# S5 lags multiplied in the third MLP from maps read back, output maps stored in place, the inputs' factors made at once, stores by token of the chunk

## The chip, the cores and the metric

The kernel runs on one core of a Trainium2 chip. The metric is the device time of one execution in microseconds (us). The kernel before was timed in 3 runs: median 1107.81 us, from 1104.62 to 1108.13.

## The reference

A decoder trunk over 256 tokens of 1024 channels in float32. Four layers, each a mixer and a squared-ReLU MLP of 4096 hidden channels, each with a norm ahead and behind:

```python
h = h + rmsnorm(mixer(rmsnorm(h, g0)), g1)
h = h + rmsnorm(mlp(rmsnorm(h, g2)), g3)      # mlp: square(relu(x @ w_up)) @ w_down
```

The mixers are a gMLP, a multi-scale pooling, a multi-head latent attention and an S5 layer. In S5, 64 groups of 16 channels each drive a complex diagonal state of 64 values:

```python
mag = exp(lr * dt); ab_re = mag * cos(li * dt); ab_im = mag * sin(li * dt)
f_re = ((ab_re - 1) * lr + ab_im * li) / den; f_im = (ab_im * lr - (ab_re - 1) * li) / den
...
# state x[t] = ab * x[t-1] + (f * B) u[t];  y = Re(C x) + d_skip * u, then gelu and a GLU
```

Nothing of `ab`, `f`, their powers or their products with B and C depends on h, so a kernel can make them any time before S5.

## The kernel before

The residual h lives in SBUF as two blocks of 128 tokens. Every float32 product is made of three float32r products of high and low halves (`mm3`, shown by the names `zhi`, `zlo`, `h1hi`, `h1lo`). The weights stream from HBM in blocks of 1 MB on SP's queue into `raw` tiles; ACT writes the high half of a block (line 338), DVE the low half (line 339), into one of 8 `w` tiles. An MLP runs a head, then 7 groups; a group is one piece of 96 matmuls up (`mm<-zhi,w`) and two of 48 down (`acc<-w,h1hi`).

The order of instructions on each engine comes from a framework that schedules the program over a simulated time with priorities. The functions below give it units of work and times. `boundary` runs a sublayer's body, its norm behind (`post`, through `add_normed`, line 391), and lifts the next sublayer's input (transposes of the scaled h on PE, line 428). In `add_normed` DVE multiplies the accumulator with the gain (`t`, line 401), ACT sums its squares (`junk`, line 352), a chain of one-column operations gives the reciprocal root, and DVE updates h (line 405).

`Tables.work()` is a generator that runs beside the sublayers from the first MLP on. It builds what S5 needs. `maps()` (from line 1675) works on POOL through 16 chunks of two pairs of groups. For each it loads B and C (`bo`), transposed B (`bt`) and powers (`pb`), multiplies B with the factors f (operations 32 wide), copies the products into `cb`, multiplies C with eight powers (`e`), negates the imaginary half, stores `e` in `d_out`, and makes the input map (`f`, stored in `d_f`). After every second chunk `lags` multiplies `e` with `cb` on PE (names `pf<-e,cb`; 16 short passes) and ACT copies the result; `place` puts the result into a Toeplitz block and stores it in `d_lag`. At the end 8 transfers copy `d_lag` into `d_m`, and 4 copy `d_out` into `d_e` (line 1724), from DRAM to DRAM. `d_m`, `d_e` and `d_f` are what S5 loads as its weights. `k.drain()` in `emit` sees that all of this has been issued before the third MLP begins.

In the third MLP `reorder` stores h (`d_h`) and loads it back in chunk order (lines 451 and 453). `finish` (line 456) stores the output: for each block two halves of 512 channels, one from SP's queue and one from ACT's, each as 4 times 32 rows of 512 channels. POOL issues all the transfers of `Tables`, of `reorder` and of the norms' gains (`bc`, line 328), in one order.

## Time and profile before

| | |
|---|---|
| runs | 1104.62, 1108.13, 1107.81 us; median 1107.81 |
| profiled execution | 1106.46 us, span of the trace 1104.7 us |
| busy: PE, DVE, ACT, POOL | 1018.0, 736.8, 548.8, 381.2 us |
| mean granted clock of PE | 0.971 of full |

The order of the sublayers in the span: gMLP; first MLP with the boundary at its start near 102 us; pooling; second MLP from 322 us; attention; third MLP from 642 us; S5; fourth MLP from 914 us. PE is TensorE, DVE VectorE, ACT ScalarE, POOL GpSimd, SP SyncE. A row of the trace's timeline has start, duration, engine, line, operation, output and inputs, the number of equal instructions in sequence, and in brackets how long the engine had been idle before and what it waited for. "Idle <-X" means that X ended last among what was waited for.

### The profile page before, as it was taken

The numbers are of one execution on the slowest core, as the hardware profiler recorded it, in microseconds if no ns is written. First come the engines' busy times: TensorE is split into PE (matmuls) and PEld (weight loads), VectorE is DVE, ScalarE is ACT, GpSimd is POOL, SyncE is SP. The second block draws the span as 40 slices with busy tenths as digits, with TensorE's granted clock in tenths as the row PEclk, the third lists the DMA queues.
The fourth block names the chain that finished last, engine by engine and source line by source line (L and its number), as shares of the span: only waits on it lengthen the run. The fifth ranks groups of instructions, "written<-read, shape, count | busy, mean of one in ns | idle before, by whom it ended". The sixth has DMA issues, their size and how long they took to land.

```text
span 1104.7 us, 16412 instructions
## 1 busy us (share of the span) xinstructions
PE 1018.0 (92%) x6408; PEld 890.3 (81%) x6409; DVE 736.8 (67%) x1099; ACT 548.8 (50%) x826; POOL 381.2 (35%) x589
## 2 busy tenths in 40 slices
PE   7898999999679998998899879999998998999994
PEld 6796999898569897986777679899966777899983
DVE  5779999754896764666876555665658577464552
ACT  5946465453454443444555455554534556444531
POOL 5000001713779999999988530000000000000000
PEclk9999999999889998999999989999999999999998
DMA  9675465758576765665864699746477554546431
GB/s 334 220 250 191 153 213 207 234 197 299 171 243 232 252 211 203 217 216 174 252 201 149 193 388 266 267 164 217 158 292 297 189 169 159 207 163 219 155 113 38
DMA packets 82607, 233.97 MB, mean 212 GB/s; under 512 B 6321, under 2 KB 9649, under 8 KB 80737
## 3 DMA queue, kind: packets, MB, share of 16 engines
q1 hardware_dynamic: 67256, 182.73, 48.4%
q0 software_dynamic: 14720, 49.60, 13.6%
q8 instruction: 50, 0.82, 0.3%
q10 hardware_dynamic: 552, 0.59, 0.1%
q14 instruction: 29, 0.23, 0.1%
HBM read 218.48 MB, written 27.00 MB: 222 GB/s over the span
## 4 chain that ended last, share of the span: by engine, by line
PE 62%; POOL 14%; DVE 11%; DMA 4%; ACT 4%; issue 3%; SPq 0%; DVEq 0%; POOLq 0%; ACTq 0%
PE mm L296 30%; PE acc L296 30%; DVE w L339 3%; DMA raw<-in_a_w_in 2%; POOL tmp L1572 2%; DMA raw<-in_w_up 1%; POOL tmp L1569 1%; DVE h L405 1%; DMA d_f<-f 1%; PE pf L296 1%; ACT junk L352 1%; PE mm L428 1%; ACT w L338 1%; DVE w L337 1%; POOL e L1704 1%
## 5 line engine op out<-in xcount | busy, mean ns | idle before, releaser
L339 DVE TENSOR_TENSOR w<-raw,w 128x1024 fp32r<-128x1024 f32 (+3 forms) x308 | 383.1, 1273 | 165.9 <-ACT w L338 164.7
L338 ACT ACTIVATE w<-raw 128x1024 fp32r<-128x1024 f32 (+3 forms) x308 | 313.1, 1044 | 232.4 <-PE acc L296 126.9
L296 PE MATMUL acc<-w,h1hi 128*128 128x512 f32 (+1 forms) x1312 | 402.5, 390 | 4.1 <-ACT h1hi L338 3.4
L296 PE MATMUL mm<-zhi,w 128*128 128x256 f32 x1920 | 358.1, 286 | 4.3 <-DVE w L337 2.4
L296 PEld LDWEIGHTS mm<-zhi,w 128*128 128x128 f32 x1920 | 305.3, 194 | 8.4 <-DVE w L337 3.5
L296 PEld LDWEIGHTS acc<-w,h1hi 128*128 128x128 f32 x1312 | 244.9, 190 | 54.1 <-ACT h1hi L338 4.7
L296 PE MATMUL mm<-zlo,w 128*128 128x256 f32 x960 | 273.6, 285 | 0.0
L296 PE MATMUL acc<-w,h1lo 128*128 128x512 f32 (+1 forms) x656 | 253.4, 391 | 1.9 <-DVE h1lo L339 1.9
L296 PEld LDWEIGHTS mm<-zlo,w 128*128 128x128 f32 x960 | 186.0, 194 | 1.5 <-issue 0.4
L296 PEld LDWEIGHTS acc<-w,h1lo 128*128 128x128 f32 x656 | 124.5, 190 | 28.9 <-DVE h1lo L339 3.3
L628 DVE TENSOR_TENSOR s<-s 128x512 f32<-128x512 f32 x56 | 42.3, 756 | 61.4 <-ACT s L627 61.4
L627 ACT ACTIVATE s<-mm 128x512 f32<-128x512 f32 x56 | 33.4, 596 | 74.0 <-PE mm L296 72.0
L339 DVE TENSOR_TENSOR h1lo<-s,h1hi 128x512 fp32r<-128x512 f32 x60 | 53.9, 900 | 21.4 <-ACT h1hi L338 21.4
L338 ACT ACTIVATE h1hi<-s 128x512 fp32r<-128x512 f32 x60 | 45.2, 756 | 27.3 <-DVE s L628 25.6
L1272 POOL MEMSET t<- 128x32 f32 x2 | 0.3, 164 | 153.0 <-DVE h L405 153.0
L352 ACT ACTIVATE junk<-acc 128x512 bf16<-128x512 f32 x28 | 16.7, 595 | 57.1 <-DVE t L401 57.0
L296 PE MATMUL mm<-w,zhi 128*128 128x512 f32 x128 | 42.1, 412 | 2.6 <-DVE zlo L339 2.1
L401 DVE TENSOR_TENSOR t<-acc,bc 128x512 f32<-128x512 f32 x28 | 19.0, 686 | 37.5 <-PE acc L296 37.5
L296 PE MATMUL acc<-w,zhi 128*128 128x512 f32 (+2 forms) x128 | 38.7, 385 | 1.6 <-ACT w L336 1.6
L428 PE MATMUL mm<-ident,t 128*128 128x128 f32 x86 | 14.6, 309 | 25.8 <-DVE t L418 21.1
L328 POOL DMA_DIRECT2D bc<-in_norm_g x15 | 8.3, 556 | 77.6 <-DVE t L401 30.5
L428 PEld LDWEIGHTS mm<-ident,t 128*128 128x128 f32 x86 | 11.4, 159 | 29.0 <-issue 27.2
(310 smaller groups left out, 1207.8 us busy)
## 6 DMA issues: line engine op xcount, KB each, us to landing
raw<-in_w_up SPq DMA_DIRECT2D x64, 1024.0 KB, 5.3
raw<-in_w_down SPq DMA_DIRECT2D x64, 1024.0 KB, 5.1
bc<-in_norm_g POOLq DMA_DIRECT2D x15, 512.0 KB, 5.2
raw<-in_a_w_in SPq DMA_DIRECT2D x7, 1024.0 KB, 9.1
bt<-in_k_bt POOLq DMA_DIRECT2D x16, 256.0 KB, 3.8
raw<-in_a_w_out SPq DMA_DIRECT2D x4, 1024.0 KB, 4.9
d_out<-e POOLq DMA_DIRECT2D x16, 256.0 KB, 2.9
d_pb<-d_pw POOLq DMA_DIRECT2D x8, 512.0 KB, 9.6
```

The lines of the kernel that those rows point to most:

```text
L296: return self.nc.tensor.matmul(out, lhsT, rhs, start=start, stop=stop)
L337: return i, nc.vector.scalar_tensor_tensor(lo, src, gain, hi.bitcast(F32), op0=ALU.mult, op1=ALU.subtract)
L338: i = nc.scalar.activation(hi, src, AF.Copy)
L339: return i, nc.vector.tensor_tensor(out=lo, in0=src, in1=hi.bitcast(F32), op=ALU.subtract)
L352: self.nc.scalar.activation(self.junk[:, 0:x.shape[-1]], x, AF.Square, scale=scale, bias=shift, accum_out=ss[:, i:i + 1])
L401: nc.vector.tensor_tensor(tn, zn, gn, op=ALU.mult)
L405: nc.vector.scalar_tensor_tensor(hn, tn, q, hn, op0=ALU.mult, op1=ALU.add)
L428: self.nc.tensor.transpose(ps[:, k * 128:(k + 1) * 128], z[:, k * 128:(k + 1) * 128], self.ident)
L627: nc.scalar.activation(s, state[f], AF.Relu)
L628: nc.vector.tensor_tensor(s, s, s, op=ALU.mult)
L1569: eng.tensor_tensor(t, xi, yi, op=ALU.mult)
L1572: eng.tensor_tensor(t, xr, yi, op=ALU.mult)
```

## The change

Four things, all at once:

1. `factors` (new) makes f·B for all chunks before `maps` starts, with eight operations on DVE, and stores it in `d_cb`. `maps` no longer makes it, nor `cb`. It multiplies C with powers that have been negated once, so that the imaginary half comes out negated; only the first 16 columns are negated afterwards. It stores `e` once for the lags (`d_ec`) and, in place of `d_out` and its four copies, with four stores straight into `d_e`.
2. `within` (new) holds lags, placement and the `d_m` transfers. It runs after `k.late` is set at the third MLP's start, and reads `e` and f·B back from `d_ec` and `d_cb` into `ec` tiles (three buffers). `drain` moves to group 6 of that MLP.
3. `add_normed` issues `sumsq` on ACT ahead of DVE's multiplies, and outside of the chain.
4. `reorder` loads h back with 4 transfers of 32 rows for each block, and `finish` stores 4 transfers of 32 rows for each half.

```diff
     def add_normed(self, b, z, g, r=None):
...
+        ss = self.sumsq(z, D ** -0.5)
         t = self.tp.tile([128, D], F32, name="t")
         for tn, zn, gn in zip(halves(t), z, halves(g)):
             nc.vector.tensor_tensor(tn, zn, gn, op=ALU.mult)
         with self.chain():
-            q = self.rstd(z, inner, outer)
+            q = self.rstd(ss, inner, outer)
...
     def reorder(self):
         for b in range(NB):
-            nc.gpsimd.dma_start(out=self.h[b], in_=in_chunks(d)[b])
+            for s in range(4):
+                nc.gpsimd.dma_start(out=self.h[b][sl32(s)], in_=in_chunks(d)[b][s])
...
     def finish(self, out):
+        nc = self.nc
         for b in range(NB):
-            o = in_chunks(out)[b] if self.chunked else out[b * 128:(b + 1) * 128]
-            for n, queue in enumerate((self.nc.sync, self.nc.scalar)):
-                queue.dma_start(out=o[..., 512 * n:512 * n + 512], in_=self.h[b][:, 512 * n:512 * n + 512])
+            for n, queues in enumerate(((nc.sync,) * 4, (nc.scalar,) * 4)):
+                c = slice(512 * n, 512 * n + 512)
+                for s, queue in enumerate(queues):
+                    queue.dma_start(out=in_chunks(out)[b][s][:, c], in_=self.h[b][sl32(s), c])
...
@@ class Mlp
     def body(self):
             k.run(self.up_units(g), side)
+            if self.i == 2 and g == 6:
+                k.drain()
...
@@ class Tables
+    def factors(self):
+        k, nc = self.k, self.nc
+        b = self.wide()
+        nc.gpsimd.dma_start(out=b, in_=self.a["k_b"])
+        br, bi = (t.rearrange("p (q c) -> p q c", c=16) for t in halves(b))
+        fr, fi = (t[:, :, None].to_broadcast([128, 32, 16]) for t in self.f)
+        for r, (x, y, op) in enumerate(((br, bi, ALU.subtract), (bi, br, ALU.add))):
+            out, w = self.wide(), self.wide()
+            u, v = (t.rearrange("p (q c) -> p q c", c=16) for t in halves(w))
+            nc.gpsimd.memset(out, 0.0)
+            nc.vector.tensor_tensor(u, x, fr, op=ALU.mult)
+            nc.vector.tensor_tensor(v, y, fi, op=ALU.mult)
+            yield 0
+            o = out.rearrange("p (q g c) -> p q g c", g=2, c=16)
+            for g in range(2):
+                hs = slice(64 * g, 64 * g + 64)
+                nc.vector.tensor_tensor(o[hs, :, g], u[hs], v[hs], op=op)
+            nc.gpsimd.dma_start(out=self.d_cb[:, r], in_=out)
+            yield 0
...
     def maps(self):
         pr, pi = self.powers
+        nr, ni = (t[:, :, 8:16] for t in (pr, pi))
+        for o, x in ((nr, pr), (ni, pi)):
+            nc.gpsimd.tensor_scalar(o, x[:, :, 0:8], -1.0, None, op0=ALU.mult)
         for ch in range(16):
-            nc.gpsimd.dma_start(out=bo[:, 0:128], in_=a["k_bc"][ch])
+            nc.gpsimd.dma_start(out=co, in_=a["k_c"][ch])
...
-            self.cmul((ov[:, 0], ov[:, 1]), (bv[:, 0], bv[:, 1]), (fb(fr), fb(fi)), tmp[:, 0:32].rearrange("p (q c) -> p q c", q=2))
-            nc.gpsimd.memset(cb, 0.0)
-            for g in range(2):
-                hs = slice(64 * g, 64 * g + 64)
-                nc.gpsimd.tensor_copy(cb[hs, :, :, g], ov[hs])
...
-            nc.gpsimd.tensor_scalar(e[:, :, 1], e[:, :, 1], -1.0, None, op0=ALU.mult)
-            nc.gpsimd.dma_start(out=self.d_out[:, qs], in_=e[:, :, :, 1:9].rearrange("p q r i c -> p q r (i c)"))
-            if made is not None:
-                self.place(lg, *made)
...
+            nc.gpsimd.tensor_scalar(e[:, :, 1, 0], cv[:, 1], -1.0, None, op0=ALU.mult)
+            nc.gpsimd.dma_start(out=self.d_ec[:, ch], in_=ec[:, 0:576])
+            for r in range(2):
+                for g in range(2):
+                    hs = slice(64 * g, 64 * g + 64)
+                    nc.gpsimd.dma_start(out=k.d_e[64 * r:64 * r + 64, 4 * ch + g:4 * ch + 4:2],
+                                        in_=e[hs, :, r, 1:9].rearrange("p q i c -> p q (i c)"))
...
-            if ch % 2:
-                with k.tc.high_priority(offset=-LATER):
-                    made = ch // 2, self.lags((before, (cb, e)))
...
+    def within(self):
+        lg = self.small("lg", 512)
+        nc.gpsimd.memset(lg, 0.0)
+        fetched = {}
+        def fetch(n):
+            fetched[n] = []
+            for ch in (2 * n, 2 * n + 1):
+                ec = k.mp.tile([128, EC], F32, name="ec")
+                nc.gpsimd.dma_start(out=ec[:, 0:576], in_=self.d_ec[:, ch])
+                nc.gpsimd.dma_start(out=ec[:, 576:EC].rearrange("p (r x) -> p r x", r=2), in_=self.d_cb[:, :, 64 * ch:64 * ch + 64])
+                fetched[n].append(self.parts_of(ec)[::-1])
+        fetch(0)
+        yield 2 * LAGS_US
+        for n in range(8):
+            t = self.lags(fetched[n])
+            if n < 7:
+                fetch(n + 1)
+            yield LAGS_US
+            self.place(lg, n, t)
+            yield LAGS_US
...
-        for r in range(2):
-            for g in range(2):
-                nc.gpsimd.dma_start(out=k.d_e[64 * r:64 * r + 64, g:64:2], in_=self.d_out[64 * g:64 * g + 64, :, r])
...
     def work(self):
+        yield from self.factors()
         yield from self.maps()
+        while not self.k.late:
+            yield 0
+        yield from self.within()
...
         if isinstance(s, Mlp) and s.i == 2:
-            k.drain()
+            k.late = True
```

How the order of instructions moves, at three places. First PE in the second MLP: an up piece of before, with passes of one lags (`pf` is the lags' accumulator in PSUM).

```order
L296 MATMUL mm<-zhi,w 128x256 x2
L296 MATMUL mm<-zlo,w 128x256
L296 MATMUL mm<-zhi,w 128x256
L296 MATMUL pf<-e,cb 32x128 x4
L296 MATMUL mm<-zhi,w 128x256
L296 MATMUL mm<-zlo,w 128x256
```

In the changed kernel the second MLP has no `pf` row. Six of the eight lags stand in the third MLP; one of them, in a down piece there, with the 8 instructions together:

```order
L298 MATMUL acc<-w,h1hi 128x512 x2
L298 MATMUL acc<-w,h1lo 128x512
L298 MATMUL pf<-ec 32x128 x8
L298 MATMUL acc<-w,h1hi 128x512 x2
L298 MATMUL acc<-w,h1lo 128x512
```

The next ones of the third MLP stand 72 up and 12 down matmuls, or 24 and 36, further on, in turn. Second, PE at the boundary into the third MLP in the changed kernel; line 431 is the lift of block 1 (line 428 before).

```order
L298 MATMUL mm<-w,zhi 128x512 x2
L298 MATMUL mm<-w,zlo 128x512
L298 MATMUL pf<-ec 32x128 x8
L431 MATMUL mm<-ident,t 128x128 x8
L431 MATMUL mm<-ident,s 128x128 x4
L298 MATMUL pf<-ec 32x128 x2
```

Lags 1 of 0 to 7 now stands right ahead of that lift, and the first passes of lags 2 behind it. Third, POOL around the store of h (`d_h`), first before:

```order
L1724 DMA d_e<-d_out 2048x128
L1573 TENSOR_TENSOR f<-f,tmp 128x4x64
L1724 DMA d_e<-d_out 2048x128 x3
L1751 DMA d_lag<-lg 128x512
L451 DMA d_h<-h_117 128x1024
L1711 DMA d_f<-f 128x512
L328 DMA bc<-in_norm_g 128x1024
L451 DMA d_h<-h_118 128x1024
```

and in the changed kernel, where rows of the last chunk of maps stand between:

```order
L454 DMA d_h<-h_118 128x1024
L1739 DMA d_ec<-ec 128x576
L1743 DMA d_e<-ec 64x2x128 x2
L1579 TENSOR_TENSOR tmp<-pb,bt 128x256
L1766 DMA ec<-d_ec 128x576
L1767 DMA ec<-d_cb 128x2x64
L1580 TENSOR_TENSOR f<-f,tmp 128x4x64
L1582 TENSOR_TENSOR tmp<-pb,bt 128x256
L330 DMA bc<-in_norm_g 128x1024
L1800 COPY lg<-lags 128x4x16
```

The copies `d_e<-d_out` are gone; the store of block 0's h now has fetches of `ec`, for lags 1 and half of lags 2, and a placement behind it.

## Rows read from the trace of the kernel before

**Rows 1.** The page's first part: busy us, share of the span, instructions.
```profile
PE 1018.0 (92%) x6408; PEld 890.3 (81%) x6409; DVE 736.8 (67%) x1099; ACT 548.8 (50%) x826; POOL 381.2 (35%) x589
```

**Rows 2.** Windows, second, third, fourth MLP: PE, PEld, DVE, ACT, POOL, PEclk, DMA, GB/s.
```profile
321.60:504.60 183.00, 174.98 (x1109) 155.13 (x1110) 111.18 (x102) 78.58 (x96) 174.36 (x257) 0.97 0.66 219
641.90:808.70 166.80, 166.80 (x1049) 152.11 (x1050) 96.53 (x105) 86.73 (x100) 9.92 (x16) 0.98 0.70 237
914.20:1079.70 165.50, 164.63 (x1048) 149.99 (x1049) 89.18 (x102) 76.96 (x93) 0.00 (x0) 1.00 0.48 166
```

**Rows 3.** Groups of PE in 321 to 505 us: busy, mean ns, idle before.
```profile
L296 PE MATMUL pf<-e,cb 128*32 128x128 f32 x64 | 5.6, 302 | 8.0 <-POOL e L1570 8.0
```

**Rows 4.** Timeline of PE: a wait in the second MLP and one in attention.
```profile
431.25 0.65 PE L296 MATMUL pf<-e,cb 128*32 128x128 f32 x8 [5.42 <-POOL e L1570]
...
520.22 0.42 PE L296 MATMUL pf<-e,cb 128*32 128x128 f32 x8 [2.99 <-POOL e L1570]
520.57 1.21 PE L296 MATMUL acc<-w,zhi 128*128 128x384 f32 x4
```

**Rows 5.** Windows behind these two waits.
```profile
431.30:435.60 4.30, 4.30 (x25) 3.92 (x26) 0.00 (x0) 0.00 (x0) 4.27 (x7) 0.50 0.64 247
521.00:524.40 3.40, 3.40 (x13) 3.40 (x12) 3.03 (x9) 0.56 (x2) 3.29 (x5) 0.50 0.79 270
```

**Rows 6.** Timeline, boundary into the third MLP: POOL, SP's queue, ACT, POOL, PE.
```profile
620.18 3.10 POOL L1724 DMA_DIRECT2D d_e<-d_out  x3
...
621.34 0.37 SPq L113 DMA_DIRECT2D raw<-in_w_up  x1
...
636.80 1.06 ACT L338 ACTIVATE w<-raw 128x1024 fp32r<-128x1024 f32 x1 [8.33 <-DMA raw<-in_w_up]
...
641.43 0.54 POOL L451 DMA_DIRECT2D d_h<-h  x1 [12.92 <-DVE h L405]
...
641.89 1.51 PE L428 MATMUL mm<-ident,t 128*128 128x128 f32 x6 [9.69 <-DVE t L418]
```

**Rows 7.** Timeline of PE, boundary into the fourth MLP.
```profile
914.24 1.01 PE L428 MATMUL mm<-ident,t 128*128 128x128 f32 x6 [2.11 <-DVE t L418]
```

**Rows 8.** DMA issues, median us to landing: whole span (2), 500 to 642, 640 to 690 us (2).
```profile
raw<-in_w_up SPq DMA_DIRECT2D x64, 1024.0 KB, 5.3
...
bt<-in_k_bt POOLq DMA_DIRECT2D x16, 256.0 KB, 3.8
...
d_e<-d_out POOLq DMA_DIRECT2D x4, 1024.0 KB, 12.0
...
d_m<-d_lag POOLq DMA_DIRECT2D x8, 512.0 KB, 13.1
...
raw<-in_w_down SPq DMA_DIRECT2D x3, 1024.0 KB, 15.5
```

**Rows 9.** Windows at the boundary into the third MLP.
```profile
626.00:636.80 10.80, 6.20 (x28) 4.81 (x26) 2.94 (x4) 2.03 (x6) 0.54 (x1) 1.00 1.00 346
636.80:647.00 10.20, 5.11 (x18) 4.55 (x19) 7.57 (x13) 5.00 (x8) 4.88 (x7) 0.51 1.03 407
```

**Rows 10.** Groups of POOL, whole span: one of the six factor operations.
```profile
L1570 POOL TENSOR_TENSOR bo<-bo,tmp 128x32 f32<-128x32 f32 x16 | 12.2, 761 | 1.2
```

**Rows 11.** Chain of waits in the third MLP: start, us, what.
```profile
663.43 10.91 PE acc L296 x48
674.34 11.51 PE mm L296 x96
```

**Rows 12.** The end: two rows of the timeline, two windows.
```profile
1091.57 0.60 ACT L352 ACTIVATE junk<-acc 128x512 bf16<-128x512 f32 x1 [2.03 <-DVE t L401]
...
1095.42 0.56 ACTq L460 DMA_DIRECT2D out<-h  x1
...
1095.40:1100.50 5.10, 0.00 (x0) 0.00 (x0) 0.00 (x0) 0.00 (x0) 0.00 (x0) 0.50 0.22 58
1100.50:1103.10 2.60, 0.00 (x0) 0.00 (x0) 0.00 (x0) 0.00 (x0) 0.00 (x0) 0.50 0.23 87
```

More of the change, by code (lines that the diff above doesn't have):

```diff
@@ L29 @@
 TURN_MAX = 0.5 - 2.0 ** -24
+EC = 704
 FMAX = float(np.finfo(np.float32).max)
@@ L40 @@
 MAPS_US = 14
+LAGS_US = 5
 LATER = 500
@@ L214, in __init__ @@
         self.recent = []
-        self.shallow = False
+        self.shallow = self.late = False
         self.weights = Weights(self)
@@ L353, in sumsq, with rstd @@
         return [ss[:, i:i + 1] for i in range(len(parts))]
-    def rstd(self, parts, inner=None, outer=None):
+    def rstd(self, sums, inner=None, outer=None):
         nc = self.nc
-        a, b = self.sumsq(parts, D ** -0.5)
+        a, b = sums
         v = self.tiny("v")
@@ L407, in factor @@
     def factor(self, b):
-        return self.rstd(halves(self.h[b]))
+        return self.rstd(self.sumsq(halves(self.h[b]), D ** -0.5))
     def scaled(self, b, g, r=None, out=None):
@@ L1456, in __init__ @@
         self.d_lag = k.dram.tile([8, 128, 512], F32, name="d_lag")
-        self.d_out = k.dram.tile([128, 32, 2, 128], F32, name="d_out")
+        self.d_ec = k.dram.tile([128, 16, 576], F32, name="d_ec")
+        self.d_cb = k.dram.tile([128, 2, 1024], F32, name="d_cb")
     def small(self, name, *shape):
@@ L1673, in spread @@
         yield 3
+    def factors(self):
[17 more added lines that the diff above has]
+            yield 0
     def maps(self):
         k, nc, a = self.k, self.nc, self.a
-        fr, fi = self.f
         pr, pi = self.powers
-        lg = self.small("lg", 512)
-        nc.gpsimd.memset(lg, 0.0)
-        before, made = None, None
+        nr, ni = (t[:, :, 8:16] for t in (pr, pi))
+        for o, x in ((nr, pr), (ni, pi)):
+            nc.gpsimd.tensor_scalar(o, x[:, :, 0:8], -1.0, None, op0=ALU.mult)
+        tt = lambda o, x, y, op: nc.gpsimd.tensor_tensor(o, x, y, op=op)
         for ch in range(16):
             qs = slice(2 * ch, 2 * ch + 2)
-            bo = self.small("bo", 192)
-            bv, ov = bo[:, 0:128].rearrange("p (n q c) -> p n q c", n=4, q=2), bo[:, 128:192].rearrange("p (n q c) -> p n q c", n=2, q=2)
+            co = self.small("bo", 64)
+            cv = co.rearrange("p (n q c) -> p n q c", n=2, q=2)
             pb, bt = self.small("pb", 2, 4, 64), self.small("bt", 2, 4, 64)
-            nc.gpsimd.dma_start(out=bo[:, 0:128], in_=a["k_bc"][ch])
+            nc.gpsimd.dma_start(out=co, in_=a["k_c"][ch])
             nc.gpsimd.dma_start(out=bt.rearrange("p r s m -> p (r s m)"), in_=a["k_bt"][ch])
@@ L1706, in maps @@
-            if made is not None:
-                self.place(lg, *made)
-                made = None
+            ec = k.mp.tile([128, EC], F32, name="ec")
+            e, _ = self.parts_of(ec)
+            er, ei = (e[:, :, r, 1:9] for r in range(2))
+            cr, ci = (cv[:, n, :, None, :].to_broadcast([128, 2, 8, 16]) for n in range(2))
+            pw = lambda t: t[:, qs, 0:8, None].to_broadcast([128, 2, 8, 16])
+            m = tmp.rearrange("p (q i c) -> p q i c", q=2, c=16)
+            tt(er, cr, pw(pr), ALU.mult)
@@ L1712, in maps, with parts_of @@
             yield MAPS_US
-            if ch % 2:
-                with k.tc.high_priority(offset=-LATER):
-                    made = ch // 2, self.lags((before, (cb, e)))
-            before = cb, e
             yield 0
-        self.place(lg, *made)
+    def parts_of(self, ec):
+        return ec[:, 0:576].rearrange("p (q r i c) -> p q r i c", q=2, r=2, c=16), ec[:, 576:EC].rearrange("p (r q g c) -> p r q g c", r=2, q=2, g=2)
+    def within(self):
+        k, nc = self.k, self.nc
+        lg = self.small("lg", 512)
[4 more added lines that the diff above has]
+            for ch in (2 * n, 2 * n + 1):
+                ec = k.mp.tile([128, EC], F32, name="ec")
+                nc.gpsimd.dma_start(out=ec[:, 0:576], in_=self.d_ec[:, ch])
[10 more added lines that the diff above has]
+            yield LAGS_US
         for i, s in enumerate(TOKEN):
@@ L1721, in maps @@
             nc.gpsimd.dma_start(out=k.d_m[16 * i:16 * i + 16], in_=w)
[L1722 to L1725 removed]
+            yield LAGS_US
     def lags(self, pairs):
```

15 lines of the change are left out of this document (8 added, 7 removed).

## The prediction

> **What bounds the kernel now.** I read the page's first part, the busy time of each stage, what PE waited for in the stages that take longest, and then those waits one at a time.
>
> PE is busy for 1018.0 us, 92% of the span [rows 1]. So only three things can shorten the kernel: less matmul work, fewer waits of PE, or less time at PE's lower clock. The three MLPs of [rows 2] do the same matmuls. The second takes 183.0 us, the third 166.8 and the fourth 165.5. The second differs in what POOL does beside it (174.36 us busy against 9.92 and 0.00), and its PE is busy 8 to 10 us longer with a mean clock of 0.97. In this stage POOL makes the maps, and PE multiplies their lags as they come. The groups name the wait: the 64 `pf<-e,cb` passes cost 8.0 us of idle time, all of it put down to a POOL instruction [rows 3]. The largest is 5.42 us; the first passes of attention wait 2.99 us in the same way [rows 4]. Behind such a wait the granted clock is 0.50, the lower of the two levels (1.2 GHz): 4.30 us behind the first wait, 3.40 behind the second [rows 5].
>
> The other place is the boundary into the third MLP. There PE waits 9.69 us [rows 6]; at the boundary into the fourth MLP it waits 2.11 [rows 7]. ACT's first split after the gap waited 8.33 us for a 1 MB weight block, issued at 621.34 and used at 636.80, so 15.5 us under way [rows 6], where the same load takes 5.3 in the median [rows 8]. Just before it POOL issued three of the four copies `d_e<-d_out`, 1 MB each, and in 626 to 636.8 us the DMA engines were busy all the time [rows 6, 8, 9]. From 636.8 to 647.0 the granted clock is 0.51 [rows 9].
>
> **The change, part by part.** The sum is made against the profiled execution, 1106.46 us, which lies 1.35 under the median of the three runs and inside their spread.
>
> a) *Lags out of the second MLP.* No row of that stage waits for POOL any more: −8.0 us of waits [rows 3]. Of 4.30 us at half clock, half is lost: −2.15 [rows 5]. Together −10.2. What is late next is the split of weights on ACT and DVE, which keeps pace in the third and fourth MLP with PE busy nearly throughout [rows 2].
>
> b) *Entry of attention.* The wait of 2.99 and half of the 3.40 at low clock are 4.7, the upper bound; the lower bound is 0, since attention waits for several engines in turn. The matmuls behind the wait start with the passes' end and wait for nothing of their own [rows 4], so I take 3.2.
>
> c) *The passes themselves.* They are moved, not removed. The 64 of the second MLP are busy for 5.6 us [rows 3], overlaps counted twice, so all 128 cost 11 us at most. They go from pooling, the second MLP and attention to the third MLP and its entry; about three quarters run inside that MLP, which gets up to 8 us longer, as the second gets up to 5.6 shorter. Sum 0 (bounds ±1, for passes that lay in a gap).
>
> d) *Boundary into the third MLP.* The 4 MB of copies go. Their bytes are now written chunk by chunk (four stores of 64 KB each), spread over the 300 us before. With the load back near 5.3 us the wait falls to that of the next boundary: 9.69 − 2.11 = 7.6. Of the low-clock stretch 641.9 to 647.0 half is lost, 2.5 [rows 6, 7, 9]. Together −10.1; lower bound −3 if the stores of h and the read-back fill the DMA engines in part.
>
> e) *POOL.* 174.36 us for eight chunks [rows 2] is 21.8 a chunk. Out go six small operations like one of 0.761 us [rows 10], two copies and the memset for `cb`, and `place` (every second chunk); the negation shrinks to a ninth of its elements; one store becomes five. That comes to about 17 us a chunk, so POOL is done with the maps before it is wanted for storing h, and is off the path. DVE's eight added multiplies and adds (at about 0.7 us each) lie at the end of the first MLP, where it waits for ACT; nothing.
>
> f) *Read-back in the third MLP.* New waits. By the order of instructions the lags follow each other 11.1 to 11.4 us apart (72 up and 12 down matmuls, or 24 and 36, at the pace of [rows 11]). With three buffers, half of a fetch can be issued only when the lags before it have been multiplied. Two issues at some 0.6 us and a landing like that of `bt`, 3.8 us for 256 KB [rows 8], are 5.0, which leaves some 6 us of margin. Nearest rows the other way: the 15.5 us landing of weights in the stretch where `d_m` and h are loaded [rows 8], which gives the first rival. What stands behind such a wait on POOL is `place`, `d_lag` and the next fetch; on PE, the up groups, which is the path. I take −2 us of my gain (0 to 46), for the two lags at the boundary.
>
> g) *`sumsq` ahead of the multiply.* ACT's `junk<-acc` waited for DVE's `t`, though it reads only the accumulator [rows 12]. In the built program it goes first and DVE follows. At eight ends of a sublayer that is 0 to 0.7 us; 0 to 6, and I take −1.5, since most of the chain is the same.
>
> h) *Last stores.* From 1095.4 to 1103.1 two stores of 256 KB move at 58 and 87 GB/s with a DMA share of 0.22 and 0.23 [rows 12], that is, on about 4 of 16 engines, and the outermost count of each store is 4. With 32 rows outermost in each I expect all 16 engines: 7.7 us become about 1.9, plus three more issues of 0.56 on the queue that ends last, 1.7 [rows 12]. −4.1 worked out; I take −3.5 (bounds +1.7, if the rate stays, and −5.8, if the issues hide).
> The Trainium skill, "DMA: Bandwidth & Descriptors", section "Why a DMA increments its semaphore by 16 and not by 1", lets the outermost count decide how many engines work, the largest divisor up to 16; by it a count of 4 gives four engines, and the trace's 0.22 agrees. The same page, "Rules for kernel authors", speaks against this part: transfers of disjoint partitions serialize and those under 64 KB are mostly overhead; by that the stores would only bring three more issues.
>
> Sum: 10.2 + 3.2 + 0 + 10.1 − 2 + 1.5 + 3.5 = 26.5 less: **1080.0 us**.
>
> **The rivals.**
>
> *1. The read-back comes late (slower).* In the third MLP the loads of h, the tables, the weights and now the maps share the DMA engines. At a landing of 15.5 us [rows 8] a fetch takes 1.2 + 15.5 = 16.7 against 11.2 between lags: 5.5 us of wait at each of six lags, 33 us, and the low clock behind each, about 2.15 as in (a), 13 more: 1080 + 46 = 1126. PE begins to wait from a landing of about 10 us, and the gain is used up (4.4 us at each lag) at about 12.3. For it: [rows 8, 9]. Against: the long landings of that stretch come from eight `d_m` transfers of 512 KB, which now follow the lags. 0.07.
>
> *2. POOL stands behind h.* The store of block 0 and of block 1 of h, and the gains' loads, sit among the fetches in POOL's order, and POOL waited 12.92 us for h there [rows 6]. If the second or third fetch is stuck so, PE waits up to that: 1080 + 12.9 = 1093. Against it: fetch 1 is issued right after block 0's h, some 15 us of matmuls ahead of its use. 0.12.
>
> *3. The second MLP is held by something else.* If the splits of weights, or POOL's denser transfers beside them, take the freed time, (a) is given back: 1090. Against: 166.8 and 165.5 us in the other two. 0.06.
>
> *4. The last stores don't spread.* If four stores of 64 KB run no wider than one, the tail grows by its three issues: +1.7 in place of −3.5, so 1085.2. For it: [rows 12] show a rate, not its cause. Inside the range; 0.10. The page's rule quoted above would give this time.
>
> *5. It doesn't shorten anything.* Rivals 2, 3 and 4 together, 12.9 + 10.2 + 5.2, give 1108. 0.05.
>
> **How the numbers follow.** The forecast has 0.60, with its own range 1067 to 1087: all upper bounds (10.2 + 4.7 + 1 + 10.1 + 6 + 5.8 = 37.8 less, no new wait) give 1069, and runs of before spread by 3.5; the boundary giving only 3 gives 1087. The range for 8 in 10 goes on to rivals 3 and 2 with some margin: 1067 to 1098. Rivals 1 and 5 are left out, 0.12, and a little beyond each end. A measurement here can tell about 0.3% from no change. Faster by more: 0.60 + 0.12 + 0.06 + 0.10 = 0.88; within it: 0.05; slower: 0.07.
>
> **What would show it.** In the profile after: the second MLP's stage at 167 to 170 us with PE's waits on POOL gone; no `pf` pass there; PE's wait at the lift into the third MLP near 2 us, its weight load near 5, the clock 1.00 behind it; the third MLP some 3 to 6 us longer through its passes, without idle time ahead of `pf<-ec`; a DMA share near 0.9 in the last stores and about 6 us from the last h to the end in place of 9.3 (from ACT's issue at 1095.42, [rows 12]). Idle time ahead of `pf<-ec` put down to the DMA or POOL, with a low clock behind it, would show rival 1 or 2; a second MLP above 178 us without `pf` passes rival 3. The prediction is wrong if the gains of (a) and (d) don't appear at their places, whatever the sum.

## The result and the profile after

The changed kernel takes 1076.3 us (median of 4 runs, 1075.72 to 1078.42) where the kernel before took 1107.85 beside it: ratio 0.9725, 95% interval 0.9703 to 0.9748. It is faster, by 31.5 us; 26.5 were forecast. Its profiled execution took 1075.72 us with a span of 1074.0, so 30.7 us are to be found between the two traces.

The first part of the page after, to be held against [rows 1]:

```profile
PE 1009.7 (94%) x6408; PEld 887.5 (83%) x6409; DVE 763.3 (71%) x1107; ACT 549.5 (51%) x826; POOL 378.2 (35%) x550
```

PE has the same 6408 instructions and 8 us less of busy time, in part through cheaper passes of the lags (below); the rest was not split further. The other 22 us were idle time of PE. POOL has 39 instructions less but almost the same busy time, and DVE has 26 us more for 8 more instructions. Both come up again below.

To see where the time went I take the start of DVE's update of h (line 405 before, 408 after; the first of each pair) as a mark at each sublayer's end, for block 0 and block 1, from the timelines.

| from ... to | before | after | difference |
|---|---|---|---|
| start, h0 behind pooling | 301.2 | 299.9 | −1.3 |
| boundary into the second MLP | 18.1 | 16.4 | −1.7 |
| second MLP | 189.8 | 172.7 | −17.1 |
| boundary into attention | 15.7 | 18.9 | +3.2 |
| attention | 90.5 | 85.9 | −4.6 |
| boundary into the third MLP | 24.4 | 16.5 | −7.9 |
| third MLP | 173.1 | 176.7 | +3.6 |
| S5, fourth MLP and their boundaries | 281.2 | 281.3 | +0.1 |
| last h to the end | 10.7 | 5.7 | −5.0 |

The second, third and fourth MLP, the first 17 us of the third and the new end in windows (columns as in [rows 2]; the first three windows go from PE's lift to the first `t` of the sublayer's end):

```profile
318.60:485.20 166.60, 166.40 (x1052) 151.67 (x1053) 126.85 (x100) 78.41 (x93) 157.93 (x194) 0.99 0.75 250
612.90:783.60 170.70, 170.39 (x1147) 152.86 (x1148) 96.48 (x104) 88.96 (x108) 43.94 (x102) 1.00 0.76 264
...
888.70:1054.80 166.10, 165.27 (x1051) 150.56 (x1052) 89.11 (x101) 77.54 (x95) 0.00 (x0) 1.00 0.48 165
...
612.90:630.00 17.10, 16.79 (x118) 15.22 (x119) 10.02 (x12) 9.30 (x12) 10.63 (x24) 1.00 1.00 310
1070.00:1072.50 2.50, 0.00 (x0) 0.00 (x0) 0.00 (x0) 0.00 (x0) 0.00 (x0) 0.50 0.74 198
```

The second MLP now takes what the fourth does, 166.6 against 166.1 us, with POOL still busy beside it for 158 of them: PE no longer waits for it. The third MLP is the longer one, 170.7, since the passes stand there, at a clock of 1.00 from its first us on. In the last stores the DMA share is 0.74 where it was 0.22 [rows 12].

PE's wait at the lift into the third MLP, and the weight load ahead of it (issues in 590 to 613 us, landing in us):

```profile
612.91 1.26 PE L431 MATMUL mm<-ident,t 128*128 128x128 f32 x8 [1.62 <-DVE t L421]
...
raw<-in_w_up SPq DMA_DIRECT2D x1, 1024.0 KB, 5.5
```

9.69 us of wait [rows 6] are 1.62, and the load lands after 5.5 us in place of 15.5.

### The profile page after: what moved, and what is told of

Its sections match the earlier page's. It is cut to its first block, busy times and chain, and to the rows that moved or that the text cites. A ratio compares the mean times of both kernels' runs of the same rounds, so it can differ in the third digit from the quotient of the medians.

```text
span 1074.0 us, 16452 instructions
## 1 busy us (share of the span) xinstructions
PE 1009.7 (94%) x6408; PEld 887.5 (83%) x6409; DVE 763.3 (71%) x1107; ACT 549.5 (51%) x826; POOL 378.2 (35%) x550
## 4 chain that ended last, share of the span: by engine, by line
PE 43%; DVE 6%; ACT 2%; issue 2%; DVEq 0%; ACTq 0%
PE acc L298 22%; PE mm L298 19%; DVE w L341 2%; PE pf L298 1%; ACT w L340 1%; DVE s L1279 0%; ACT s L1150 0%; DVE h L408 0%; DVE s L1158 0%; DVE t L404 0%; PE mm L431 0%; DVE zlo L341 0%; DVE h1lo L341 0%; DVE t L421 0%; DVE s L1006 0%
## 5 line engine op out<-in xcount | busy, mean ns | idle before, releaser
L341 DVE TENSOR_TENSOR w<-raw,w 128x1024 fp32r<-128x1024 f32 (+3 forms) x308 | 398.0, 1322 | 143.3 <-ACT w L340 141.7
L635 DVE TENSOR_TENSOR s<-s 128x512 f32<-128x512 f32 x56 | 44.9, 801 | 41.1 <-ACT s L634 41.0
L1715 POOL TENSOR_TENSOR ec<-bo,pr 128x256 f32<-128x256 f32 x32 | 35.0, 1110 | 27.5 <-DVE pr L1648 23.5
L1743 POOL DMA_DIRECT2D d_e<-ec x64 | 39.9, 628 | 0.0
L298 PEld LDWEIGHTS acc<-w,zhi 128*128 128x128 f32 x128 | 25.5, 208 | 9.3 <-ACT zhi L340 4.1
```

Source lines behind the costliest of these rows:

```text
L298: return self.nc.tensor.matmul(out, lhsT, rhs, start=start, stop=stop)
L341: return i, nc.vector.tensor_tensor(out=lo, in0=src, in1=hi.bitcast(F32), op=ALU.subtract)
L635: nc.vector.tensor_tensor(s, s, s, op=ALU.mult)
L1715: tt = lambda o, x, y, op: nc.gpsimd.tensor_tensor(o, x, y, op=op)
L1743: nc.gpsimd.dma_start(out=k.d_e[64 * r:64 * r + 64, 4 * ch + g:4 * ch + 4:2], in_=e[hs, :, r, 1:9].rearrange("p q i c -> p q (i c)"))
```

## The experiments

Eleven kernels. Each was timed against the kernel before on its own chip, so ratios are the surer comparison; differences of times are told beside them. A kernel with a change in its program gets a new order of instructions from the framework on all engines. Only experiments 1 and 2 keep the order of the kernel that they start from; in the others the new order is part of what was measured. Times of places are from one trace of each kernel.

**1. The last stores alone.** The kernel before with the new `finish` and nothing else; the order of all other work stays.

```diff
-            for n, queue in enumerate((self.nc.sync, self.nc.scalar)):
-                queue.dma_start(out=o[..., 512 * n:512 * n + 512], in_=self.h[b][:, 512 * n:512 * n + 512])
+            for n, queues in enumerate(((nc.sync,) * 4, (nc.scalar,) * 4)):
+                c = slice(512 * n, 512 * n + 512)
+                for s, queue in enumerate(queues):
+                    queue.dma_start(out=in_chunks(out)[b][s][:, c], in_=self.h[b][sl32(s), c])
```

> The kernel before with the new last stores alone (four stores of 32 rows for each half). Theory: in the changed kernel the last h begins 5.7 us ahead of the span's end, before it was 10.7, so the stores alone give 5.0 us, wherever else time goes: 1102.8 us, DMA share above 0.4 in the last 4 us. Rival: the shorter end comes from what precedes the stores (the order of ACT and DVE); then this run stays within 1.5 us of 1107.9.

Ratio 0.9966 (0.9946 to 0.9986), 1.6 to 6.0 us less. In its profile the last h begins at 1092.50 and the span ends at 1098.3, so 5.8 us where it was 10.7: 4.9 us. A window in the stores:

```profile
1094.50:1096.50 2.00, 0.00 (x0) 0.00 (x0) 0.00 (x0) 0.00 (x0) 0.00 (x0) 0.50 0.85 225
```

The term stands by itself, and the theory held.

**2. Two stores of 64 rows for each half.** The changed kernel with the outermost count 2; the instructions of PE, DVE and POOL keep their order.

```diff
-                for s, queue in enumerate(queues):
-                    queue.dma_start(out=in_chunks(out)[b][s][:, c], in_=self.h[b][sl32(s), c])
+                for s in range(2):
+                    queue.dma_start(out=in_chunks(out)[b][2 * s:2 * s + 2][..., c], in_=self.h[b][64 * s:64 * s + 64, c])
```

> The changed kernel with the last stores as two of 2x32 rows for each half instead of four of 32. Theory: the outermost count of a store sets how many DMA engines it uses; with 2 the rate falls to half of that with 4, the stores take some 14 us where they took 7.2 before the change, and the span ends about 18 us behind the last h in place of 5.7: 1088 us, DMA share about 0.12. Rival: the size of a store decides; 128 KB lies between 64 and 256, so 1076 to 1079 us and a share between 0.23 and 0.5.

1087.44 us (1085.41 to 1088.72), ratio 0.9824 (0.9804 to 0.9845). The span ends 16.1 us behind the last h (1070.95 to 1087.0). A window in its stores:

```profile
1073.00:1085.00 12.00, 0.00 (x0) 0.00 (x0) 0.00 (x0) 0.00 (x0) 0.00 (x0) 0.50 0.13 51
```

0.13 is 2 of 16. So 2, 4 and 32 as the outermost count give a share of 0.13, 0.22 and 0.74 to 0.85, while the size of a store (128, 256, 64 KB) stands in another order. The Trainium skill, "DMA: Bandwidth & Descriptors", section "Why a DMA increments its semaphore by 16 and not by 1", lets the number of engines follow from the outermost count, and here the trace agrees. The prediction holds a row of "Rules for kernel authors" against the split, on the same page of the Trainium skill. That row gives as its reason that both halves already use all 16 engines; the stores of before did not (share 0.22), so it does not bear on them. Another row of that section of the Trainium skill confines a transfer to as many engines as its outermost count when that is below 16, as seen here. The split has a price of its own: the four issues take 1.75 us on ACT's queue, and the share stays below 1.

**3. The output maps in place, alone.** The kernel before, with four stores into `d_e` in every chunk for `d_out`, and without the four copies.

```diff
-            nc.gpsimd.dma_start(out=self.d_out[:, qs], in_=e[:, :, :, 1:9].rearrange("p q r i c -> p q r (i c)"))
+            for r in range(2):
+                for g in range(2):
+                    hs = slice(64 * g, 64 * g + 64)
+                    nc.gpsimd.dma_start(out=k.d_e[64 * r:64 * r + 64, 4 * ch + g:4 * ch + 4:2],
+                                        in_=e[hs, :, r, 1:9].rearrange("p q i c -> p q (i c)"))
...
-        for r in range(2):
-            for g in range(2):
-                nc.gpsimd.dma_start(out=k.d_e[64 * r:64 * r + 64, g:64:2], in_=self.d_out[64 * g:64 * g + 64, :, r])
```

> The kernel before with the output maps stored straight into their place by four stores in every chunk, without the four late copies. Theory: PE's wait at the lift into the third MLP falls from 9.7 to 2 to 4 us and the weight load there from 15.5 to about 6 us, some 8 to 10 us less at that place; POOL gets three more issues of 0.63 us in each of 16 chunks, so the lags come later and PE's waits for POOL in the second MLP and attention grow by 2 to 10 us; total 1098 to 1106. Rival: the copies were not what delayed the boundary; then PE's wait there stays above 7 us and the total above 1107.

Ratio 0.9902 (0.9865 to 0.9939). PE's wait at the lift:

```profile
623.33 1.08 PE L428 MATMUL mm<-ident,t 128*128 128x128 f32 x4 [4.21 <-DVE t L418]
```

The wait falls by 5.5 us to 4.2, a little above what was expected, and the boundary by 6.2 (24.4 to 18.2). The other half of the expectation failed. PE's waits for POOL in the second MLP did not grow but fell, to 4.4 us with the first passes counted, though POOL has more to do: the framework had put the passes elsewhere. POOL's speed alone does not tell where PE waits. The trace is that of the fastest run, 1090.96 us, where the next one took 1099.22; the ratio is the surer figure for the whole.

**4. The copies back, late.** The changed kernel with `d_out` again and the four copies right behind the store of block 0's h. (A dependency on that store fixes the place; in the changed kernel POOL waits 10.59 us for this h.)

```diff
             first = nc.gpsimd.dma_start(out=d[b * 128:(b + 1) * 128], in_=self.h[b])
+            if not b:
+                with self.after([first.ins]):
+                    for r in range(2):
+                        for g in range(2):
+                            nc.gpsimd.dma_start(out=self.d_e[64 * r:64 * r + 64, g:64:2], in_=self.d_out[64 * g:64 * g + 64, :, r])
```

> The changed kernel with the output maps stored in one piece again and the four copies of 1 MB issued by POOL right behind the store of block 0's h, the place at which they stood before. All else is kept. Theory: the copies delay the weight load at the boundary; its landing goes back above 12 us, PE's wait at the lift into the third MLP from 1.6 to 7 to 10 us with low clock behind, 1084 to 1088 us. Rival: the other parts of the change (POOL done earlier, the order of the sum of squares) shortened the boundary; then PE's wait stays below 4 us and the time at 1075 to 1079.

1099.74 us (1095.71 to 1100.24), ratio 0.9929 (0.9904 to 0.9954): 23 us more than the changed kernel, far beyond both. At the boundary the theory held: it takes 23.5 us in place of 16.5, and PE waits 8 us in three pieces. The longest is for ACT's copy of lags, which stands behind a split for whose weight block ACT waited 9.30 us; such loads land after 13.8 us there:

```profile
632.13 1.18 PE L298 MATMUL pf<-ec 128*32 128x128 f32 x16 [6.01 <-ACT lags L1795]
634.38 0.64 PE L298 MATMUL pf<-ec 128*32 128x128 f32 x4 [1.07 <-ACT lags L1795]
635.91 1.32 PE L431 MATMUL mm<-ident,t 128*128 128x128 f32 x5 [0.89 <-DVE t L421]
...
d_e<-d_out POOLq DMA_DIRECT2D x4, 1024.0 KB, 13.2
raw<-in_w_up SPq DMA_DIRECT2D x3, 1024.0 KB, 13.8
```

Of the rest some 12 us arise in attention, where the new order had put passes of the lags; PE waited there 3.83 and 1.29 us for maps read back, at 553 and 558 us. POOL issues the copies only at 612, so that part is the order's, not the copies'.

**5. The lags back in the maps' loop.** The changed kernel without `within`: passes and `place` as in the kernel before, f·B read from `d_cb`, `e` stored in place.

```diff
             yield MAPS_US
+            if ch % 2:
+                with k.tc.high_priority(offset=-LATER):
+                    made = ch // 2, self.lags((before, (cb, e)))
+            before = cb, e
...
-        while not self.k.late:
-            yield 0
-        yield from self.within()
```

> The changed kernel with the lags multiplied inside the maps' loop again (factors still made by VectorE, output maps still stored in place). Theory: where the lags stand decides; POOL's chunk is about 19 us, PE's passes stand where a faster POOL would have them, so PE waits for POOL again by 4 to 10 us in the second MLP with half clock behind: 1082 to 1092. Rival: POOL's shorter chunk alone took the waits away; then 1073 to 1078, without waits ahead of the passes.

1087.82 us (1084.44 to 1090.74), ratio 0.9818 (0.9793 to 0.9843). The marks put 11.5 us on the second MLP (184.2), −4.5 on the third (172.2), and nothing on the boundary into the third (16.8). Windows of the second MLP between the marks, of this kernel and of the changed one, and the group of its passes:

```profile
317.90:502.10 184.20, 177.40 (x1132) 156.24 (x1133) 123.12 (x113) 83.40 (x108) 167.16 (x220) 1.00 0.67 225
...
L298 PE MATMUL pf<-ec 128*32 128x128 f32 x64 | 6.2, 285 | 3.3 <-POOL ec L1712 3.2
```

```profile
316.30:489.00 172.70, 170.25 (x1068) 154.91 (x1069) 132.24 (x113) 82.43 (x104) 162.89 (x204) 0.99 0.74 246
```

So the waits are back with 3.3 us, a bit less than expected, and the mean clock of the stage stays at 1.00; what I had not expected is that 64 passes, in pieces of two to eight, make PE busy for 7.2 us longer, while the third MLP gives back only 4.5 for its 112. The boundary stays short without the late copies, which tells the two gains apart.

**6. The old order in `add_normed`.** The changed kernel with `sumsq` behind the multiplies.

```diff
-        ss = self.sumsq(z, D ** -0.5)
         t = self.tp.tile([128, D], F32, name="t")
...
-            q = self.rstd(ss, inner, outer)
+            q = self.rstd(self.sumsq(z, D ** -0.5), inner, outer)
```

> The changed kernel with the sum of squares emitted behind the multiplies again. Theory: the two still follow each other on the accumulator, in either order; from the first of them to the first operation of the chain it is 1.51 us before and 1.33 after, 0.18 at each of eight ends, so +1.4 us over the changed kernel's 1076.3: 1077.7. Rival: the order hides a whole multiply of 0.69 at each end, +5.5: 1081.8.

1082.59 us (1079.31 to 1089.83), ratio 0.9784 (0.9754 to 0.9814). Against the changed kernel's 0.9725 that is 2 to 10 us more, nearer to the rival, though not by its mechanism: at the end of the fourth MLP the first operation and the chain are 1.51 us apart (1070.98 to 1072.49), as the theory says. Of the 6.0 us between the two traces 2.4 arise ahead of the first h behind pooling, 2.1 in attention, 1.5 in S5 and the fourth MLP, and 1.5 at the boundary into the second MLP; the other places give 1.5 back. Only the last of these was followed to its rows, DVE:

```profile
313.19 0.68 DVE L403 TENSOR_TENSOR t<-acc,bc 128x512 f32<-128x512 f32 x1
313.79 5.30 DVE L341 TENSOR_TENSOR w<-raw,w 128x1024 fp32r<-128x1024 f32 x2
319.01 0.32 DVE L363 TENSOR_SCALAR v<-ss 128x1 f32<-128x1 f32 x2
```

Two splits of weights stand between the multiply and the chain, as in the kernel before. With the new order the chain comes right behind (the boundary takes 16.4 us in place of 17.9).

**7. The new order alone.** The kernel before with that edit only.

> The kernel before with the sum of squares emitted ahead of the multiplies and outside of the chain, and nothing else. Theory: what undoing it cost in the changed kernel (6 us, by the boundary into the second MLP and those behind it) is what it gives here too: 1101 to 1103. Rival: its worth hangs on the rest of the change, as the order of all engines is made anew; 1106 to 1110.

1111.29 us (1103.74 to 1115.12), ratio 1.0032 (1.0009 to 1.0054): no gain, and by the interval a loss of 1 to 6 us, so the rival, a little beyond its times. The passes were moved by the new order, and PE waited for POOL twice at length in the second MLP:

```profile
430.87 0.43 PE L296 MATMUL pf<-e,cb 128*32 128x128 f32 x8 [4.82 <-POOL e L1571]
...
480.93 0.66 PE L296 MATMUL pf<-e,cb 128*32 128x128 f32 x8 [4.21 <-POOL e L1571]
```

All its waits for POOL there are 9.6 us, where the kernel before has 8.0. That is 1.6 of the 6.4 us by which this trace is longer; 3.7 arise in attention, where the wait for POOL is the same 2.98, and why was not settled. So the worth of this edit is no term of its own: it gained inside the changed kernel and lost in the kernel before.

**8. A multiply in the chain's gap.** The changed kernel with the second multiply emitted behind ACT's square root.

```diff
         nc.scalar.activation(s, v, AF.Sqrt)
+        if between is not None:
+            between()
```

> The changed kernel with the second multiply of the accumulator by the gain placed behind the square root's request, where VectorE waits for ACT. Theory: of its 0.6 us 0.3 are hidden in that wait, at eight ends of a sublayer: 2.4 us less, 1074. Rival: VectorE's order elsewhere changes with it, and a split of weights takes the place ahead of the chain, as in the second MLP's boundary of the kernel before: 1077 to 1082.

1079.68 us (1077.88 to 1084.0), ratio 0.9762 (0.9734 to 0.9789). Slower than the changed kernel's ratio by some 0.4%, though the intervals overlap, and inside the rival's 1077 to 1082. The gain did not appear, and the trace, which is that of the slowest run, shows one reason: at the ends of the MLPs the multiply does not stand in the gap. The framework put it between the chain's first two operations, ahead of the square root, and the gap of 0.27 stays empty. DVE at the end of the fourth MLP:

```profile
1074.39 0.27 DVE L365 TENSOR_SCALAR v<-ss,r 128x1 f32<-128x1 f32 x1 [2.03 <-ACT junk L354]
1074.58 0.68 DVE L408 TENSOR_TENSOR t<-acc,bc 128x512 f32<-128x512 f32 x1
1075.18 0.14 DVE L366 TENSOR_SCALAR v<-v 128x1 f32<-128x1 f32 x1
1075.60 0.15 DVE L376 TENSOR_SCALAR v<-v 128x1 f32<-128x1 f32 x1 [0.27 <-ACT sq L373]
```

So the theory was tested only at other ends, where the chain has no such second operation. At the lift into the third MLP PE's transposes wait 1.07 and 0.66 us, 1.73 for the 1.62 of the changed kernel, yet the clock drops behind them (0.53 in 617 to 622 us); what decides that is not shown.

**9. No arithmetic in the maps.** The changed kernel with two memsets in each chunk in place of POOL's fourteen operations; its maps are zero, so the S5 layer's part of the output is left out.

> The changed kernel with POOL's arithmetic of the maps replaced by two memsets in each chunk (the maps are then zero); all transfers stay. Theory: POOL's arithmetic slows VectorE's weight splits beside it (mean 1.67 us in the second MLP against 1.22 in the third), and the split that ACT waits for at the entry of attention took 3.27 us for that reason; here the mean is 1.22 to 1.25, PE's wait there falls from 3.7 to below 2 us, and the time to 1070 to 1074. Rival: the order on ACT sets that wait; it stays above 3 us and the time at 1075 to 1078.

1062.84 us (1060.66 to 1063.47), ratio 0.9599 (0.9576 to 0.9622): 13.5 us less than the changed kernel, more than expected. By the marks: boundary into the second MLP 13.4 in place of 16.4, second MLP 174.3 and no gain, boundary into attention 13.0 in place of 18.9, attention 81.0 in place of 85.9. The wait at the entry of attention is gone. VectorE's splits of 1024 columns in the second MLP take 1.22 us in the mean, as expected, and VectorE is busy for 12.7 us in the boundary into attention in place of 18.8, and for 55.1 in attention in place of 65.7. The chain of tiny operations on DVE in the entry of attention, in the changed kernel (with the row of POOL beside it) and in this one:

```profile
505.85 0.15 DVE L375 RECIPROCAL r<-sq 128x1 f32<-128x1 f32 x1
506.03 1.44 DVE L377 SCALAR_TENSOR_TENSOR tn<-v,r 128x1 f32<-128x1 f32 x1
...
506.25 1.20 POOL L1715 TENSOR_TENSOR ec<-bo,pr 128x256 f32<-128x256 f32 x2
```

```profile
500.23 0.15 DVE L375 RECIPROCAL r<-sq 128x1 f32<-128x1 f32 x1
500.42 0.22 DVE L377 SCALAR_TENSOR_TENSOR tn<-v,r 128x1 f32<-128x1 f32 x1
```

The same operation on one column takes 1.44 us beside POOL's arithmetic and 0.22 without; it ends at 507.47, and POOL's two operations at 507.45. PE is busy through the second MLP either way. That the slowed chains at boundaries and in attention are the whole of the 13.5 us is not shown: without its arithmetic POOL also issues its transfers earlier, and the order on PE and DVE is a new one, with no lag passes in attention.

**10. A part of the maps on VectorE.** The changed kernel with the six operations that make `f` on DVE.

```diff
-            self.cmul([f[:, :, r] for r in range(2)], (pb[:, 0], pb[:, 1]), (bt[:, 0], bt[:, 1]), tmp.rearrange("p (s m) -> p s m", s=4))
+            self.cmul([f[:, :, r] for r in range(2)], (pb[:, 0], pb[:, 1]), (bt[:, 0], bt[:, 1]), tmp.rearrange("p (s m) -> p s m", s=4), nc.vector)
```

> The changed kernel with the six operations of each chunk that make the input map (f) on VectorE in place of POOL. Theory: POOL's arithmetic beside VectorE costs time, most of it in attention and at its entry (without it the kernel takes 1063); with some 5 us less in each chunk POOL ends the maps before attention, so attention and its entry shorten by 8 to 12 us, and VectorE's 35 us more lie in the second MLP, where it idles; 1064 to 1069 us. Rival: VectorE's added work stands ahead of the weight splits in the second MLP, and PE waits there; 1076 to 1085.

1071.91 us (1070.9 to 1074.13), ratio 0.9693 (0.9666 to 0.972). Between the two expectations, and by its median the fastest whole kernel here, some 0.3% below the changed one's ratio, with intervals that overlap a little. The boundary into attention shortens by 3.7 us (15.2) and that into the third MLP by 2.0; the second MLP gets 3.2 longer. Attention itself stays at 86.2, though POOL was idle for most of it:

```profile
507.50:593.70 86.20, 79.14 (x470) 69.14 (x469) 58.80 (x129) 46.39 (x103) 11.13 (x18) 0.92 0.52 172
```

A wait of 3.66 us ahead of 525 us and a clock of 0.50 from 525 to 533 stand there (2.85 us, and 523 to 528.5, in the changed kernel), and 16 lag passes where the changed kernel has 4. VectorE is 6.9 us less busy in attention than in the changed kernel, and attention is no shorter, so being rid of its slowed operations there did not shorten the stage in this order. What set the wait was not tried further.

**11. Each map read back three times.**

```diff
-                nc.gpsimd.dma_start(out=ec[:, 0:576], in_=self.d_ec[:, ch])
+                for _ in range(3):
+                    nc.gpsimd.dma_start(out=ec[:, 0:576], in_=self.d_ec[:, ch])
```

> The changed kernel with each map for the lags read back three times into the same tile. Theory: a fetch ends 8 to 9 us after the lags before it (2.6 us of issues and 6.2 of landing) with 12 us between lags, so 3 us of room; four more issues of 0.6 us and 1.2 MB more transfer per pair use that up, and PE waits 0 to 4 us ahead of each of six lags: 1077 to 1095, with idle time of PE ahead of pf. Rival: there is much more room (a fetch is early by a whole lag); then no wait and 1075 to 1078.

1085.82 us (1085.5 to 1088.18), ratio 0.9821 (0.9794 to 0.9847). The time lies in the range of the theory, but not for its reason: PE never waits ahead of `pf`. The framework knows of the transfers and puts the passes later and apart; the last stand at 776 us in place of 707, and the `d_m` transfers at 781 in place of 714. The cost is paid behind the third MLP (5.5 of the 12.5 us between the traces), where operands of S5 come late, and in the third MLP (4.8), where the passes cost 2.4 more in smaller pieces (two and six instructions by the order, eight in the changed kernel). S5's wait, and the passes' group in the third MLP of this kernel and of the changed one:

```profile
832.42 0.89 PE L298 MATMUL mm<-raw,zlo 128*32 128x128 f32 x12 [2.40 <-DMA raw<-d_f]
...
L298 PE MATMUL pf<-ec 128*32 128x128 f32 x112 | 7.3, 282 | 0.0
```

```profile
L298 PE MATMUL pf<-ec 128*32 128x128 f32 x112 | 4.9, 279 | 0.0
```

So the room of the read-back at the present places was not measured by this run; the trace of the changed kernel shows it, below.

## Why the prediction was right, and where it was wrong

By place, the second and third MLP gave 13.5 us where the terms (a), (c), (f) and the clock of (d) come to 10.7; the entry of attention and attention 1.4 for 3.2; the boundary into the third MLP 7.9 for 7.6; the end 5.0 for 3.5; the start and the boundary into the second MLP 3.0, where only (g) had entered 1.5. So most gains came at their places. The sum is nearer than its terms, since (b) fell short while the others went beyond: that part is luck.

*(a) and (c), the lags out of the second MLP: right, a little small.* Forecast were 10.2 us and up to 5.6 for the passes; the marks show 17.1. Experiment 5 takes 11.5 of it back when the lags return, with waits of 3.3 us. The step "sum 0" for the passes was mis-sized. [rows 3] have 5.6 us for 64 passes, 87 ns each, in pieces of eight passes and fewer; in the third MLP, most of them sixteen together, they take 4.9 us for 112 (the group shown under experiment 11), 44 ns each. By an estimate from these rows the move saved about 64 × 43 ns = 2.8 us by that. In pooling, which the prediction left out of (a), PE's waits for POOL went too, but the next operand was no earlier, so nothing was gained there. PE before, and after:

```profile
294.30 0.64 PE L296 MATMUL pf<-e,cb 128*32 128x128 f32 x4 [3.25 <-POOL e L1704]
296.01 4.19 PE L296 MATMUL mm<-raw,t 128*128 128x128 f32 x22 [1.07 <-DVE t L420]
```

```profile
295.85 1.44 PE L298 MATMUL mm<-raw,t 128*128 128x128 f32 x5 [5.60 <-DVE t L423]
```

*(b), entry of attention: wrong.* The wait for POOL went, but that the matmuls behind it "wait for nothing of their own" did not hold in the new order. The entry, where all that (b) counted lies, got 3.2 us longer where I took 3.2 off. Attention got 4.6 shorter; that was not (b)'s, and how much of it comes of the 32 lag passes that left attention (36 before, 4 after) is not shown. The rows, ACT before; PE, ACT, DVE and POOL after:

```profile
516.73 0.57 ACT L338 ACTIVATE zhi<-mm 128x512 fp32r<-128x512 f32 x1
```

```profile
500.08 1.27 PE L298 MATMUL acc<-w,zhi 128*128 128x384 f32 x3 [3.66 <-ACT zhi L340]
...
498.54 1.00 ACT L340 ACTIVATE w<-raw 128x960 fp32r<-128x960 f32 x1 [2.38 <-issue]
499.45 0.58 ACT L340 ACTIVATE zhi<-mm 128x512 fp32r<-128x512 f32 x1
...
495.19 3.27 DVE L341 TENSOR_TENSOR w<-raw,w 128x768 fp32r<-128x768 f32 x1
...
495.54 0.74 POOL L1578 TENSOR_TENSOR f<-pb,bt 128x256 f32<-128x256 f32 x1
496.24 0.72 POOL L1581 TENSOR_TENSOR f<-pb,bt 128x256 f32<-128x256 f32 x1
496.92 0.71 POOL L1715 TENSOR_TENSOR ec<-ec,tmp 128x256 f32<-128x256 f32 x1
```

After, PE waits for `zhi`, ACT's `zhi` stands behind a split of 960 columns that starts right after DVE's split ends, and that split of 768 columns took 3.27 us beside three operations of POOL; the next one took 0.94. Before, the first `zhi` was written at 517.3, 2.9 us ahead of the passes of [rows 4], so this wait was not in line behind the removed one: it is new. Experiment 9, without POOL's arithmetic, has no wait there.

*(d), boundary into the third MLP: right.* Forecast 7.6 and 2.5. The boundary is 7.9 shorter, the load lands after 5.5 us, and the clock behind the lift is 1.00. Experiments 3 and 4 show the copies as the cause from both sides (6.2 us less alone, 7 more when put back). In experiment 3 the wait of 4.2 is above the changed kernel's 1.6, and the clock behind it is 0.50 (623.3 to 630 us), so not all of it is the copies'.

*(e), POOL: half wrong.* It is off PE's direct path, as forecast: it waits 10 us for h0. But its chunk takes 19.5 us (the stores of `d_f` in the second MLP, from 373.0 to 490.25 in six steps), not 17, since the operations that remain got slower: those of 256 columns take 1.04 us in the mean of this stage, 0.84 before. And "off the path" overlooked what POOL does to DVE. Experiment 9 gives 13.5 us for all of POOL's arithmetic, with POOL's own time and a new order in the figure; experiment 10, with six of the fourteen operations moved to DVE, gained some 4 by the medians, with intervals that overlap.

*(f), read-back: right in kind, 2 us too dear.* No pass in the third MLP waits. Rival 1 did not come. POOL, one round of it:

```profile
647.38 0.60 POOL L1766 DMA_DIRECT2D ec<-d_ec  x1 [16.24 <-PE pf L298]
...
649.25 0.71 POOL L1767 DMA_DIRECT2D ec<-d_cb  x1
...
659.70 0.59 POOL L1766 DMA_DIRECT2D ec<-d_ec  x1 [7.41 <-PE pf L298]
...
ec<-d_ec POOLq DMA_DIRECT2D x9, 288.0 KB, 6.5
```

From the lags at 647 to the last issue 2.6 us, then 6.5 to landing (the median of issues from 640 to 760 us, not the 3.8 of `bt`), so some 3 us of room in the 12 between two lags, where I had 6. The added passes and the clock give 3.6 us more in the third MLP, as forecast.

*(g), the sum of squares: the step did not hold.* The 1.5 us would be eight times 0.18. Experiments 6 and 7 show 2 to 10 us with the rest of the change, which reaches beyond the bound of 6, and a loss of 1 to 6 without it, where the lower bound was 0. What the framework puts between multiply and chain is a part of it; most of either figure has no cause shown.

*(h), last stores: right, small.* 5.0 us by the marks and 4.9 alone, for 3.5 taken and 4.1 worked out (the 9.3 that the prediction names for the old end counts from ACT's issue; from the last h it was 10.7). Experiment 2 shows the outermost count as the cause, and rival 4 fell.

Of the rivals, 2 did not come either: POOL waited 10 us for h0, yet the second fetch was in time. Rival 3 has something in it, not in the second MLP but at the entry of attention.

## What to carry to other kernels

Look at the outermost count of every last store: few rows there mean few DMA engines, and the end of the kernel is where that is not hidden. When a wait is removed, read when the next operand arrives, and read it again in the new order: in pooling it came no earlier, and at the entry of attention a new wait took back the gain. And count arithmetic on POOL as a possible cost to VectorE's chains, also where no engine waits for POOL's results.

## What the runs showed of the hardware

VectorE's operations are slowed beside POOL's arithmetic one at a time, not evenly. In the second MLP the mean of a weight split of 1024 columns is 1.43 us before and 1.67 after, and 1.22 in the third and fourth. The softmax's multiply of two SBUF operands in attention takes 1.24 us beside POOL's arithmetic and 0.69 without, while the scores' operation, which reads PSUM, takes 0.69 in both. Groups of DVE in attention, of the changed kernel and of experiment 9:

```profile
L1158 DVE TENSOR_TENSOR s<-s,smx 128x512 f32<-128x512 f32 x6 | 7.4, 1241 | 0.1
...
L1143 DVE TENSOR_TENSOR s<-mm,cap 128x512 f32<-128x512 f32 x6 | 4.0, 686 | 4.8 <-PE mm L298 4.8
```

```profile
L1158 DVE TENSOR_TENSOR s<-s,smx 128x512 f32<-128x512 f32 x6 | 4.1, 689 | 0.1
L1143 DVE TENSOR_TENSOR s<-mm,cap 128x512 f32<-128x512 f32 x6 | 4.0, 686 | 5.1 <-PE mm L298 5.1
```

The Trainium skill, "SBUF — State Buffer", section "SBUF: two separate sides", says that a VectorE operation with two SBUF inputs and a POOL operation that reads SBUF hold a port for the whole instruction while the other waits; the rows agree, down to a one-column operation with two SBUF inputs that takes 1.44 us and ends with POOL's operations, while the reciprocal ahead of it, with one input, takes 0.15 in both kernels (experiment 9). A pass of the lags makes PE busy for 44 ns where most stand sixteen together, 65 in experiment 11 and 87 in pieces of eight and fewer (the group's busy time over its count, overlaps with neighbours included).
